# An RWKV-7 loop on TensorE: the source's order in turns, small tiles ahead of full ones, recurrence steps in two halves

## The chip, the cores and the metric

The kernel runs on one core of a Trainium2 chip. The metric is the device time of one execution in microseconds (us), as a median over runs. Two small networks are computed one after the other: a first block of two layers (an RWKV-7 mixer and a gated delta-rule mixer, each with a gated feed-forward part) and a second block of two layers. The change touches only the RWKV-7 mixer of the first layer, which takes about 280 us of the 2128 us span.

## The reference

For 256 tokens, a width of 1024 and 16 heads of 64, cut to what matters:

```python
r, k, v = lerp(0) @ w_rkv[0], lerp(1) @ w_rkv[1], lerp(2) @ w_rkv[2]
w_log = -softplus(-(w0 + tanh(lerp(3) @ w1) @ w2)) - 0.5
a = sigmoid(a0 + (lerp(4) @ a1) @ a2)
g = sigmoid(lerp(5) @ g1) @ g2
kk = l2norm(heads(k * k_k));  k = k * (1 + (a - 1) * k_a)
decay = exp(-exp(w_log))

def step(S, inp):                       # over the tokens, per head, S is 64x64
    sa = einsum('bhvk,bhk->bhv', S, a_t)            # a_t = -kk, b_t = kk * a
    S = S * w_t + sa * b_t + v_t * k_t
    return S, einsum('bhvk,bhk->bhv', S, r_t)

y = group_norm(y) * gn_g + gn_b;  y = (y + sum(r * k * r_k) * v) * g
return y @ w_out
```

The kernel does the recurrence in chunks of 64 tokens: within a chunk a triangular 64x64 matrix is inverted, and only the state S goes from chunk to chunk.

## The kernel before

The 16 heads are 8 pairs, p = 0 to 7. A pair fills 128 partitions, one head on rows 0 to 63 and one on rows 64 to 127, and its 256 tokens are 4 chunks. Each pair passes five stages, written as Python generators in `rwkv` (line numbers of before):

- `project(p)`: k, r and v of the pair, 24 matmuls of 128x128 by 256 each, all into the one PSUM bank `pj`; ScalarE copies a finished sum out (`ksb`, `rsb`, `vsb`, L1059) before the next may start. Each weight block arrives as f32, ScalarE casts its high half `wh` and VectorE subtracts for the low half `wl`.
- `stage_a(p)`: gates, norms and decays, mostly on VectorE and ScalarE, with single matmuls into the one bank `pt` (`lo0`, `kq`, `pr`), then four pairs of transposes into the same bank (`bh`, `kh`, `ah`, `vsb` against `ident`, L1136). After each pair four copies take the bank out (`bt`, `kt`, `at`, `vt`, L1143), in turn by VectorE, ScalarE, VectorE and ScalarE. Last come the products of 64x64 tiles into bank `G` (L1158).
- `stage_b(p)`: the inverse of the triangular matrices in 10 rounds, each 8 matmuls of 64x64 tiles into one of two banks `B` (L906) followed by one VectorE operation that the next round reads (`ivz` L921 or `ivx` L932), then three more products (`akv`, `WT`, `U`).
- `stage_c(p)`: the recurrence over 4 chunks. Per chunk `C<-st,WT` (L1201), VectorE's `sa` (L1203), products into `S` and `C` that read `sa`, and VectorE's new state `st` (L1217, L1221); then the group norm and the gate (`y`, `yq`, `lo1`).
- `early()`: the output projection over the pairs 0 to 5 (L1326), and `tail()`: vectors for later layers (`onecol`, `adacc`).

`run_spread` interleaves the generators: each has a number of steps and a start and end in units of one pair, and the generator whose next step is due first runs up to its next `yield`. A scheduler then takes these instructions in the program's order as priority and orders each engine's queue by its own estimate of durations, TensorE's too. Each engine runs its queue strictly in that order. A tile of a PSUM bank may be written again only when all reads of its last content are done.

TensorE works with two kinds of tile here: full ones (128 rows) and 64x64 ones, on which the two heads of a pair sit in two corners. The short products of `lo0` use 64 rows by 128 columns. Each f32 matmul stands in the trace as two records, so that a round of 8 matmuls is "x16" there.

Of the kernel before, what the change touches and what calls it, by code (L numbers as in the profile page):

```python
# [18 lines left out]
NCH = 8  # L19
# [732 lines left out]

def run_spread(*gens):

    live = [[g, n, a, b, 0] for g, n, a, b in gens]
    while live:
        e = min(live, key=lambda e: e[2] + (e[3] - e[2]) * (e[4] + 1) / e[1])
        try:
            next(e[0])
            e[4] += 1  # L760
        except StopIteration:
            live.remove(e)


class First:
# [174 lines left out]
    def rwkv(self):  # L940
        n, nc, P, T = self.n, self.n.nc, self.n.P, T1
        tc = n.tc
        with ExitStack() as es:
# [102 lines left out]
            def project(c, names="krv"):  # L1046
                for nm in names:
                    L = {"k": Lk, "r": Lr, "v": Lv}[nm]
                    ps = n.ps("pj", T)
                    w = n.wblock("r" + nm, c)  # L1050
                    for k in range(NCH):
                        wh, wl = w(k)
                        with tc.issue_after(self.anchor) if self.anchor is not None and k % 2 < 0 else nullcontext():
                            for i, (a, b) in enumerate(((wh, L[k][0]), (wh, L[k][1]), (wl, L[k][0]))):
                                nc.tensor.matmul(ps, a, b, start=(k == 0 and i == 0), stop=(k == 7 and i == 2))  # L1055
                        if k < 7 and nm not in "":
                            yield
                    o = st[c][nm] = t_(nm + "sb", 2)
                    nc.scalar.copy(o, ps)  # L1059
                    yield  # L1060

            def stage_a(c):
# [5 lines left out]
                for i, nm in enumerate(("SW", "AI")):  # L1068
                    w = slice(64 * i, 64 * i + 64)
                    ps = n.ps("pt", T)  # L1070
                    n.mm3([ps], [lambda k: tuple(q[w] for q in wa2)], [tuple(q[w] for q in lo[0])])
                    t = t_(nm)
                    sigmoid(t, ps, hc[:, i * 8 + c:i * 8 + c + 1])
                    SA.append(t)
                SW, A = SA
                yield
                q = t_("kq")
# [7 lines left out]
                nc.vector.scalar_tensor_tensor(kk, d["k"], P("k_k", c), rn, op0=MUL, op1=MUL)  # L1085
                yield
                cs = t_("cs")
# [16 lines left out]
                nc.scalar.activation(E0, dp, AF.Exp, scale=-KP)  # L1104
                yield
                kp_ = t_("kp")
# [13 lines left out]
                d["AR"] = AR4  # L1120
                yield
                r, v = d["r"], d["v"]
                nc.vector.tensor_tensor(AR4[:, :, 1], c4(r), c4(E1), op=MUL)
                pr = t_("pr")
                nc.vector.scalar_tensor_tensor(pr, r, P("r_k", c), kp_, op0=MUL, op1=MUL)
                yield
                ps = n.ps("pt", T)
                nc.tensor.matmul(ps, bo, pr, start=True, stop=True)
                bv = d["bv"] = r_(6, "bv")
                nc.vector.scalar_tensor_tensor(bv, ps, 64.0, v, op0=MUL, op1=MUL)  # L1130
                yield

# [13 lines left out]
                tok(lambda J: bh[:, ts(J, 128)], "bt", 2)  # L1146
                yield
                tok(lambda J: kh[:, ts(J, 128)], "kt", 2)
                yield
                tok(lambda J: ah[:, ts(J, 128)], "at", 2)  # L1150
                yield
                tok(lambda J: v[:, ts(J, 128)], "vt", 3)
# [16 lines left out]
            def stage_b(c):  # L1169
# [13 lines left out]

                akv = mm(d["Ak"], d["vt"], "akv")
                d["WT"] = mm(d["at"], XT, "WT")
                yield
# [3 lines left out]
            def stage_c(c):  # L1190
                d = st[c]
                yp = n.ps("S", T)
                S = None
                for j in range(4):
                    cj = ts(j, 64)
# [8 lines left out]
                    for r in H:  # L1204
                        nc.tensor.matmul(yp[r, cj], d["vt"][r, cj], d["Rk"][r, cj], start=True, stop=False)
                        if S is not None:
                            nc.tensor.matmul(yp[r, cj], S[r], d["AR"][r, j, 1], start=False, stop=False)
                        anchor = nc.tensor.matmul(yp[r, cj], sa[r], d["Rb"][r, cj], start=False, stop=True).ins
                    if j < 3:
                        ps = n.ps("C", 64)  # L1210
                        for r in H:
                            nc.tensor.matmul(ps[r], d["kt"][r, cj], d["vt"][r, cj], start=True, stop=False)
                            nc.tensor.matmul(ps[r], d["bt"][r, cj], sa[r], start=False, stop=True)
                        S2 = t_("st", 2, 64)
                        fj = d["f"][:, j:j + 1]
# [6 lines left out]
                        S = S2  # L1222
                    yield
                y = t_("y")
                nc.scalar.copy(y, yp)
                ps = n.ps("S", T)
                nc.tensor.matmul(ps, bo, y, start=True, stop=True)
                nc.vector.tensor_tensor(y, y, ps, op=SUB)
                q = t_("yq")
                nc.scalar.activation(q, y, AF.Square)  # L1230
                ps = n.ps("S", T)
                nc.tensor.matmul(ps, bo, q, start=True, stop=True)
                nc.scalar.activation(q, ps, AF.Ln, bias=n.consts[64e-5])
                nc.scalar.activation(q, q, AF.Exp, scale=-0.5)
                nc.vector.scalar_tensor_tensor(y, y, P("gn_g", c), q, op0=MUL, op1=MUL)
                yield
                nc.vector.scalar_tensor_tensor(y, y, P("gn_b", c), d["bv"], op0=ADD, op1=ADD)
# [5 lines left out]
                n.split_to(*yo[c], y)  # L1243
                yield

# [19 lines left out]
            def after(g, key, *needs):  # L1265
                for q in needs:
                    while q not in have:
                        yield
                yield from g()
                have.add(key)  # L1270


            def tail():
                for _ in more:
                    yield
                have.add("more")

            da, oa, la = 1, 0.0, 1.285
            ob, lb, oc, lc = 1.108, 1.0, 1.886, 0.963
            of, lf, oe, le = 0.1, 1.272, 7.918, 2.446  # L1280
            om, lm = 0.247, 8.0
            have.add(("f", 0))
            run_spread((tail(), 8 * len(self.PARTS[0]) + 1, om, om + lm),
                       *((after(lambda p=p: project(p), ("f", p), ("f", p - 1)), 24, p - 1 + of, p - 1 + of + lf) for p in range(1, NCH)),
                       *((after((lambda p=p: stage_a(p)) if p else (lambda: first), ("a", p), ("f", p)), 12, p + oa, p + oa + la) for p in range(NCH)),
                       *((after(lambda p=p: stage_b(p), ("b", p), ("a", p)), 12, p + ob, p + ob + lb) for p in range(NCH)),
                       *((after(lambda p=p: stage_c(p), ("c", p), ("b", p)), 6, p + oc, p + oc + lc) for p in range(NCH)),
                       (after(early, "e", "more", ("a", 7), ("c", 5)), 56, oe, oe + le))
            xs = new_x("s{}h")
# [617 lines left out]
```

## Time and profile before

| | |
|---|---|
| median of 3 runs (lowest, highest) | 2125.14 us (2124.67, 2127.45) |
| the profiled execution, its span | 2129.63 us, 2127.8 us |
| TensorE busy over the span | 2066.7 us, 97% |
| VectorE, ScalarE busy | 1449.8 us (68%), 1102.5 us (52%) |
| share of TensorE in the chain that ended last | 86% |
| DMA, mean | 159 GB/s |

A busy TensorE is not one at its peak: the ends of matmuls are modelled, and a short wait between two of them can vanish inside a busy stretch. So the starts of neighbouring matmuls are the better measure, and the text reads those.

### The profile page before, as it was taken

What the parts mean: (1) busy time and instruction counts of PE and PEld (TensorE: products, weight loads), DVE (VectorE), ACT (ScalarE), POOL (GpSimd) and SP (SyncE); (2) the same over time, 40 slices, a digit from 0 to 9 for tenths busy, and PEclk for the clock granted to TensorE, in tenths of its full rate; (3) what the DMA queues carried; (4) which work ended last, traced back from release to release, by engine and by line L of the source; (5) the groups of instructions that cost most, each with busy time, mean ns of one, the idle gap of its engine ahead of it and who ended that gap; (6) DMA issues with size and microseconds to landing.
All of it is one profiled execution on the core that took longest, in us unless ns stands there. A gap on an engine that the chain in (4) does not pass through costs nothing.

```text
span 2127.8 us, 43221 instructions
## 1 busy us (share of the span) xinstructions
PE 2066.7 (97%) x17602; PEld 1913.9 (90%) x17602; DVE 1449.8 (68%) x2959; ACT 1102.5 (52%) x2057; POOL 29.1 (1%) x68
## 2 busy tenths in 40 slices
PE   7999999999999999999999999999999999999998
PEld 6888888999888989999999876899999998779998
DVE  7878876887788867656555776755565457767555
ACT  4544445444745556545454744644454537456443
POOL 0000000000011100000000000000000000000000
PEclk9999999999999999999999999999999999999999
DMA  7524323896534337655554331455455443225553
GB/s 272 166 85 124 103 66 101 322 316 224 184 129 131 103 105 244 204 172 179 188 176 161 135 99 55 134 187 171 163 167 186 165 166 132 90 70 178 189 179 120
DMA packets 102087, 337.30 MB, mean 159 GB/s; under 512 B 11456, under 2 KB 19456, under 8 KB 101888
## 3 DMA queue, kind: packets, MB, share of 16 engines
q1 hardware_dynamic: 101888, 334.54, 47.2%
q8 instruction: 138, 2.26, 0.4%
q14 instruction: 61, 0.50, 0.1%
HBM read 333.45 MB, written 1.05 MB: 157 GB/s over the span
## 4 chain that ended last, share of the span: by engine, by line
PE 86%; DVE 6%; ACT 4%; DMA 2%; issue 1%; POOL 0%; SPq 0%; ACTq 0%; DVEq 0%; POOLq 0%
PE pj L157 17%; PE pj L158 17%; PE pj L160 17%; PE pj L128 9%; PE pj L1055 4%; PE B L906 2%; DVE wl L101 2%; PE yp L585 1%; PE B L1354 1%; PE pj L148 1%; DMA wr<-in_ffn_in_dram 1%; PE G L1158 1%; PE pj L149 1%; PE pj L152 1%; PE sy L638 1%
## 5 line engine op out<-in xcount | busy, mean ns | idle before, releaser
L101 DVE TENSOR_TENSOR wl<-wr,wh 128x1024 fp32r<-128x1024 f32 (+2 forms) x557 | 640.7, 1160 | 290.6 <-ACT wh L100 140.9
L100 ACT CAST wh<-wr 128x1024 fp32r<-128x1024 f32 (+2 forms) x557 | 555.0, 1002 | 495.6 <-PE pj L158 209.2
L266 DVE TENSOR_TENSOR hh<-sg,pj 128x256 f32<-128x256 f32 (+1 forms) x132 | 56.4, 428 | 147.4 <-PE pj L160 127.2
L817 DVE SCALAR_TENSOR_TENSOR adacc<-adar,cond,adacc 128x512 f32<-128x512 f32 x140 | 104.2, 744 | 11.3 <-DMA adar<-in_ada_dram 9.7
L177 ACT ACTIVATE q<-r 128x256 f32<-128x256 f32 (+1 forms) x80 | 33.1, 423 | 95.2 <-DVE r L198 71.1
L157 PE MATMUL pj<-s0h,wh 128*128 128x256 f32 (+1 forms) x240 | 68.4, 285 | 0.9 <-ACT wh L100 0.9
L160 PE MATMUL pj<-s6h,wl 128*128 128x256 f32 (+1 forms) x240 | 68.6, 286 | 0.0
L158 PE MATMUL pj<-s5l,wh 128*128 128x256 f32 (+1 forms) x240 | 68.4, 285 | 0.0
L157 PE MATMUL pj<-s6h,wh 128*128 128x256 f32 (+1 forms) x240 | 68.4, 285 | 0.0
L158 PE MATMUL pj<-s7l,wh 128*128 128x256 f32 (+1 forms) x240 | 68.3, 285 | 0.0
L160 PE MATMUL pj<-s1h,wl 128*128 128x256 f32 (+1 forms) x240 | 68.3, 284 | 0.0
L160 PE MATMUL pj<-s5h,wl 128*128 128x256 f32 (+1 forms) x240 | 68.2, 284 | 0.0
L160 PE MATMUL pj<-s7h,wl 128*128 128x256 f32 (+1 forms) x240 | 68.2, 284 | 0.0
L160 PE MATMUL pj<-s0h,wl 128*128 128x256 f32 (+1 forms) x240 | 68.2, 284 | 0.0
L160 PE MATMUL pj<-s4h,wl 128*128 128x256 f32 (+1 forms) x240 | 68.2, 284 | 0.0
L157 PE MATMUL pj<-s4h,wh 128*128 128x256 f32 (+1 forms) x240 | 68.2, 284 | 0.0
L158 PE MATMUL pj<-s1l,wh 128*128 128x256 f32 (+1 forms) x240 | 68.1, 284 | 0.0
L160 PE MATMUL pj<-s2h,wl 128*128 128x256 f32 (+1 forms) x240 | 68.1, 284 | 0.0
L158 PE MATMUL pj<-s3l,wh 128*128 128x256 f32 (+1 forms) x240 | 68.0, 284 | 0.0
L157 PE MATMUL pj<-s7h,wh 128*128 128x256 f32 (+1 forms) x240 | 68.0, 284 | 0.0
L157 PE MATMUL pj<-s1h,wh 128*128 128x256 f32 (+1 forms) x240 | 68.0, 283 | 0.0
L157 PE MATMUL pj<-s5h,wh 128*128 128x256 f32 (+1 forms) x240 | 68.0, 283 | 0.0
(1660 smaller groups left out, 7294.5 us busy)
## 6 DMA issues: line engine op xcount, KB each, us to landing
wr<-in_ffn_in_dram SPq DMA_DIRECT2D x264, 512.0 KB, 3.9
wr<-in_ffn_out_dram SPq DMA_DIRECT2D x96, 512.0 KB, 3.5
adar<-in_ada_dram SPq DMA_DIRECT2D x80, 512.0 KB, 4.6
wr<-in_w_in_dram SPq DMA_DIRECT2D x40, 512.0 KB, 3.4
wr<-in_ffn_out_dram SPq DMA_DIRECT2D x48, 384.0 KB, 3.6
wr<-in_gin_dram SPq DMA_DIRECT2D x32, 512.0 KB, 3.5
ada<-in_ada_dram SPq DMA_DIRECT2D x16, 512.0 KB, 7.4
wr<-in_w_out_dram SPq DMA_DIRECT2D x16, 512.0 KB, 3.5
```

The source lines that it names most:

```text
L100: nc.scalar.copy(h, r)
L101: nc.vector.tensor_tensor(l, r, h.bitcast(F32), op=SUB)
L128: mm(o, a, b[:, t0:], start=(c == 0), stop=(c == 23))
L148: mm(o, wh, xs[k][0], start=(i == 0), stop=False)
L157: mm(o, wh, xs[k][0], start=(i == 0), stop=False)
L158: mm(o, wh, xs[k][1], start=False, stop=False)
L160: mm(o, w(k)[1], xs[k][0], start=False, stop=(i == K - 1))
L177: nc.scalar.activation(q[k], d[k], AF.Square)
L266: nc.vector.tensor_tensor(hh, sg, up, op=MUL)
L817: nc.vector.scalar_tensor_tensor(acc, r[:, ts(k, 512)], c, acc, op0=MUL, op1=ADD)
L906: self.anchor = nc.tensor.matmul(out[r, c], lhsT[r, c], rhs[r, c], start=start, stop=start or b == nblk - 1).ins
L1055: nc.tensor.matmul(ps, a, b, start=(k == 0 and i == 0), stop=(k == 7 and i == 2))
```

## The change

Four things change. TensorE's queue in the loop is no longer ordered by the scheduler but stands as the source emits it (`manual_schedule`). `run_spread` gets `turns=12`: due times are rounded down to twelfths of a pair, and within one such turn the generators whose next step is marked as one of 64x64 tiles (a plain `yield` before it) run ahead of those marked `yield True` (full tiles). Steps are cut anew: a recurrence chunk becomes two steps, with `sa` between them, and the group norm and the first part of `stage_a` are cut into more steps. And the products with `kt` and `vt` use bank `dm` in place of `C` for the pairs 0 to 5. The number of matmuls stays the same.

```diff
-def run_spread(*gens):
-
-    live = [[g, n, a, b, 0] for g, n, a, b in gens]
+def run_spread(*gens, turns=None):
+    live = [[g, n, a, b, 0, None] for g, n, a, b in gens]
+    at = lambda e: e[2] + (e[3] - e[2]) * (e[4] + 1) / e[1]
     while live:
-        e = min(live, key=lambda e: e[2] + (e[3] - e[2]) * (e[4] + 1) / e[1])
+        e = min(live, key=at if turns is None else lambda e: (math.floor(at(e) * turns), e[5] is not None))
         try:
-            next(e[0])
+            e[5] = next(e[0])
             e[4] += 1
...
                         if k < 7 and nm not in "":
-                            yield
+                            yield True
...
+                    if i == 0:
+                        yield True
                 SW, A = SA
-                yield
+                yield True
...
                 akv = mm(d["Ak"], d["vt"], "akv")
+                yield
                 d["WT"] = mm(d["at"], XT, "WT")
...
+                other = "dm" if c < 6 else "C"
...
-                        anchor = nc.tensor.matmul(yp[r, cj], sa[r], d["Rb"][r, cj], start=False, stop=True).ins
                     if j < 3:
-                        ps = n.ps("C", 64)
+                        ps = n.ps(other, 64)
                         for r in H:
                             nc.tensor.matmul(ps[r], d["kt"][r, cj], d["vt"][r, cj], start=True, stop=False)
+                    if S is not None:
+                        yield
+                    for r in H:
+                        if j < 3:
                             nc.tensor.matmul(ps[r], d["bt"][r, cj], sa[r], start=False, stop=True)
+                    for r in H:
+                        nc.tensor.matmul(yp[r, cj], sa[r], d["Rb"][r, cj], start=False, stop=True)
...
-                    yield
+                    yield True if j == 3 else None
                 y = t_("y")
                 nc.scalar.copy(y, yp)
+                yield True
...
-            ob, lb, oc, lc = 1.108, 1.0, 1.886, 0.963
+            ob, lb, oc, lc = 1.108, 13 / 12, 1.886, 1.0
...
+            with tc.manual_schedule(engines={mybir.EngineType.PE}):
+                run_spread(*((after(lambda p=p: stage_c(p), ("c", p), ("b", p)), 12, p + oc, p + oc + lc) for p in range(NCH)),
+                           *((after(lambda p=p: stage_b(p), ("b", p), ("a", p)), 13, p + ob, p + ob + lb) for p in range(NCH)),
+                           *((after((lambda p=p: stage_a(p)) if p else (lambda: first), ("a", p), ("f", p)), 13, p + oa, p + oa + la) for p in range(NCH)),
+                           *((after(lambda p=p: project(p), ("f", p), ("f", p - 1)), 24, p - 1 + of, p - 1 + of + lf) for p in range(1, NCH)),
+                           (tail(), 8 * len(self.PARTS[0]) + 1, om, om + lm),
+                           (after(early, "e", "more", ("a", 7), ("c", 5)), 56, oe, oe + le), turns=12)
```

Three places of TensorE's queue show the order. A row is a line of the kernel, the operation, out<-in by the names above, and the size of the result; line numbers of the changed kernel are 3 to 17 higher. The first place is the middle of the loop, around pair 3, where the recurrence and the inverse of neighbouring pairs run beside `project`. Before:

```order
L1080 MATMUL pt<-kq,bo 128x256
L906 MATMUL B<-ivz,ivt 64x64 x8
L1055 MATMUL pj<-s4l,wh 128x256
L1055 MATMUL pj<-s4h,wl 128x256
L1205 MATMUL S<-Rk,vt 64x64
L1055 MATMUL pj<-s5h,wh 128x256
L1201 MATMUL C<-st,WT 64x64 x2
L1207 MATMUL S<-AR,st 64x64
L1055 MATMUL pj<-s5l,wh 128x256
L906 MATMUL B<-ivx,MT 64x64 x8
L1055 MATMUL pj<-s5h,wl 128x256
```

The same stage with the change:

```order
L1208 MATMUL C<-st,WT 64x64 x2
L1212 MATMUL S<-Rk,vt 64x64
L1214 MATMUL S<-AR,st 64x64
L1212 MATMUL S<-Rk,vt 64x64
L1214 MATMUL S<-AR,st 64x64
L909 MATMUL B<-ivx,MT 64x64 x8
L1058 MATMUL pj<-s6h,wh 128x256
L1058 MATMUL pj<-s6l,wh 128x256
L1058 MATMUL pj<-s6h,wl 128x256
L1225 MATMUL S<-Rb,sa 64x64 x2
L909 MATMUL B<-ivz,ivt 64x64 x8
L1058 MATMUL pj<-s7h,wh 128x256
```

Before, the kind of tile changes 8 times in 11 rows, now 3 times in 12: the 64x64 rows of a turn stand together. The second place is the pair of transposes of `kh` and the next, of `ah`, into the same bank `pt`, for pair 3. Before:

```order
L1136 MATMUL pt<-ident,kh 128x128 x2
L1055 MATMUL pj<-Mset,wh 128x256
L906 MATMUL B<-ivt,ivz 64x64 x8
L1179 MATMUL B<-vt,Ak 64x64 x8
L1055 MATMUL pj<-Mset,wl 128x256
L1179 MATMUL B<-ivt,at 64x64 x7
L1136 MATMUL pt<-ident,ah 128x128 x2
```

And now, with the rows that follow:

```order
L1141 MATMUL pt<-ident,kh 128x128 x2
L1058 MATMUL pj<-L6h,wh 128x256
L1058 MATMUL pj<-L6l,wh 128x256
L1058 MATMUL pj<-L6h,wl 128x256
L909 MATMUL B<-ivx,MT 64x64 x8
L1141 MATMUL pt<-ident,ah 128x128 x2
L1058 MATMUL pj<-L7h,wh 128x256
L1058 MATMUL pj<-L7l,wh 128x256
L1058 MATMUL pj<-L7h,wl 128x256
L1058 MATMUL pj<-Mset,wh 128x256 x2
```

Between the two pairs of transposes 25 rows' worth of matmuls stood (23 small, 2 full), and 11 stand there now (8 small, 3 full). The last two rows are the third place: the sum of r ends with `L7h,wl` and that of v begins with `Mset,wh`, into the one bank `pj`, with nothing between. Before, the same border of pair 3 was:

```order
L906 MATMUL B<-ivx,MT 64x64 x8
L1055 MATMUL pj<-L7h,wl 128x256
L1158 MATMUL G<-AR,bh 64x128 x3
L1055 MATMUL pj<-Mset,wh 128x256 x2
L1158 MATMUL G<-AR,bh 64x128 x2
```

Three products into `G` stood between the two sums there. Over the whole loop, from the first `lo0` row to the last `lo1` row, the kind of tile on TensorE changes 344 times before and 263 times with the change.

## Rows read from the trace of the kernel before

**Rows 1.** Windows, the loop: length, busy us (instructions) of each engine, granted clock, DMA share.
```profile
51.70:334.30 282.60, 277.54 (x3524) 230.49 (x3523) 221.05 (x585) 133.39 (x342) 0.00 (x0) 0.99 0.35 111
```

**Rows 2.** Timeline of TensorE: start, length, line, out<-in, tile, count; two rounds.
```profile
316.21 0.28 PE L1326 MATMUL pt<-yo0l,wh 128*128 128x256 f32 x1
316.42 0.68 PE L906 MATMUL B<-ivt,ivz 64*64 64x64 f32 x16
316.93 0.63 PE L1179 MATMUL B<-vt,Ak 64*64 64x64 f32 x16
317.49 0.39 PE L1326 MATMUL pt<-yo0h,wl 128*128 128x256 f32 x1
317.71 0.28 PE L1326 MATMUL pt<-yo1h,wh 128*128 128x256 f32 x1
317.83 0.28 PE L1326 MATMUL pt<-yo1l,wh 128*128 128x256 f32 x1
```

**Rows 3.** Timeline of TensorE, a recurrence chunk between full tiles.
```profile
321.33 0.28 PE L1326 MATMUL pt<-yo4h,wl 128*128 128x256 f32 x1
321.54 0.33 PE L1201 MATMUL C<-st,WT 64*64 64x64 f32 x4
321.70 0.28 PE L1205 MATMUL S<-Rk,vt 64*64 64x64 f32 x2
321.82 0.28 PE L1207 MATMUL S<-AR,st 64*64 64x64 f32 x2
322.02 0.38 PE L1326 MATMUL pt<-yo5h,wh 128*128 128x256 f32 x1
322.25 0.28 PE L1326 MATMUL pt<-yo5l,wh 128*128 128x256 f32 x1
```

**Rows 4.** Timeline of all engines, one round of the inverse; brackets: idle before, releaser.
```profile
161.09 0.68 PE L906 MATMUL B<-ivx,MT 64*64 64x64 f32 x16
...
161.82 0.42 DVE L921 TENSOR_TENSOR ivz<-B,rc 128x256 f32<-128x256 f32 x1 [0.23 <-PE B L906]
...
163.98 0.42 DVE L932 TENSOR_TENSOR ivx<-B,ivx 128x256 f32<-128x256 f32 x1
...
164.46 0.54 PEld L906 LDWEIGHTS B<-ivx,MT 64*64 64x64 f32 x14 [0.34 <-DVE ivx L932]
```

**Rows 5.** Groups of VectorE, 75 to 330 us: count, busy us, mean ns, idle before.
```profile
L921 DVE TENSOR_TENSOR ivz<-B,rc 128x256 f32<-128x256 f32 x40 | 16.8, 421 | 7.0 <-PE B L906 6.8
...
L1203 DVE TENSOR_TENSOR sa<-C,U 128x64 f32<-128x64 f32 x24 | 5.2, 218 | 5.8 <-PE C L1201 5.5
...
L1221 DVE SCALAR_TENSOR_TENSOR st<-C,f,sf 128x64 f32<-128x64 f32 x16 | 4.5, 282 | 7.4 <-PE C L1213 7.2
```

**Rows 6.** Timeline, bank pt between the transposes of kh and ah.
```profile
166.69 0.38 PE L1136 MATMUL pt<-ident,kh 128*128 128x128 f32 x2
...
167.45 0.28 DVE L1143 COPY kt<-pt 64x128 f32<-64x128 f32 x1
167.76 0.26 ACT L1143 COPY kt<-pt 64x128 f32<-64x128 f32 x1 [2.71 <-DVE kt L1143]
168.30 0.29 DVE L1143 COPY kt<-pt 64x128 f32<-64x128 f32 x1
168.71 0.26 ACT L1143 COPY kt<-pt 64x128 f32<-64x128 f32 x1
...
169.11 0.44 PE L1136 MATMUL pt<-ident,ah 128*128 128x128 f32 x2
```

**Rows 7.** Timeline, bank pj between the sums of r and v.
```profile
161.70 0.39 PE L1055 MATMUL pj<-L7h,wl 128*128 128x256 f32 x1
...
162.12 0.37 ACT L1059 COPY rsb<-pj 128x256 f32<-128x256 f32 x1 [2.78 <-PE pj L1055]
...
162.59 0.19 PEld L1055 LDWEIGHTS pj<-Mset,wh 128*128 128x128 f32 x1 [0.17 <-ACT rsb L1059]
```

**Rows 8.** Windows, a stretch at a lower granted clock.
```profile
132.00:140.00 8.00, 8.00 (x75) 6.40 (x76) 3.99 (x9) 1.60 (x5) 0.00 (x0) 0.57 0.24 76
```

More of the change, by code (lines that the diff above doesn't have):

```diff
@@ L1085, in stage_a @@
                 nc.vector.scalar_tensor_tensor(kk, d["k"], P("k_k", c), rn, op0=MUL, op1=MUL)
-                yield
+                yield True
                 cs = t_("cs")
@@ L1104, in stage_a @@
                 nc.scalar.activation(E0, dp, AF.Exp, scale=-KP)
-                yield
+                yield True
                 kp_ = t_("kp")
@@ L1120, in stage_a @@
                 d["AR"] = AR4
-                yield
+                yield True
                 r, v = d["r"], d["v"]
@@ L1125, in stage_a @@
                 nc.vector.scalar_tensor_tensor(pr, r, P("r_k", c), kp_, op0=MUL, op1=MUL)
-                yield
+                yield True
                 ps = n.ps("pt", T)
@@ L1130, in stage_a @@
                 nc.vector.scalar_tensor_tensor(bv, ps, 64.0, v, op0=MUL, op1=MUL)
-                yield
+                yield True
                 def tok(src, name, bufs):
@@ L1146, in stage_a @@
                 tok(lambda J: bh[:, ts(J, 128)], "bt", 2)
-                yield
+                yield True
                 tok(lambda J: kh[:, ts(J, 128)], "kt", 2)
-                yield
+                yield True
                 tok(lambda J: ah[:, ts(J, 128)], "at", 2)
-                yield
+                yield True
                 tok(lambda J: v[:, ts(J, 128)], "vt", 3)
@@ L1207, in stage_c @@
                             nc.tensor.matmul(yp[r, cj], S[r], d["AR"][r, j, 1], start=False, stop=False)
[L1208 removed]
                     if j < 3:
[L1210 removed]
+                        ps = n.ps(other, 64)
                         for r in H:
                             nc.tensor.matmul(ps[r], d["kt"][r, cj], d["vt"][r, cj], start=True, stop=False)
+                    if S is not None:
+                        yield
+                    for r in H:
+                        if j < 3:
                             nc.tensor.matmul(ps[r], d["bt"][r, cj], sa[r], start=False, stop=True)
+                    for r in H:
+                        nc.tensor.matmul(yp[r, cj], sa[r], d["Rb"][r, cj], start=False, stop=True)
+                    if j < 3:
                         S2 = t_("st", 2, 64)
@@ L1222, in stage_c @@
                         S = S2
-                    yield
+                    yield True if j == 3 else None
                 y = t_("y")
                 nc.scalar.copy(y, yp)
+                yield True
                 ps = n.ps("S", T)
@@ L1230, in stage_c @@
                 nc.scalar.activation(q, y, AF.Square)
+                yield True
                 ps = n.ps("S", T)
@@ L1235, in stage_c @@
                 nc.vector.scalar_tensor_tensor(y, y, P("gn_g", c), q, op0=MUL, op1=MUL)
-                yield
+                yield True
                 nc.vector.scalar_tensor_tensor(y, y, P("gn_b", c), d["bv"], op0=ADD, op1=ADD)
@@ L1243, in stage_c @@
                 n.split_to(*yo[c], y)
-                yield
+                yield True
             gk, gr, gv = lerps(1, "s", Lk), lerps(0, "L", Lr), lerps(2, "M", Lv)
@@ L1282, in rwkv @@
             have.add(("f", 0))
[L1283 to L1288, printed above, removed]
+            with tc.manual_schedule(engines={mybir.EngineType.PE}):
[5 more added lines that the diff above has]
+                           (after(early, "e", "more", ("a", 7), ("c", 5)), 56, oe, oe + le), turns=12)
             xs = new_x("s{}h")
```

## The prediction

> **What bounds the kernel now.** The change stays inside the RWKV loop, so I read the windows first: from the first `lo0` row to the last `lo1` row is 51.8 to 334.2 us, 282.4 us in which TensorE is busy 277.5 us, VectorE 221 and ScalarE 133 [rows 1]. TensorE sets this stretch; VectorE, at 78%, is not far behind. But a busy TensorE is not one at its peak, so I then read the timeline by starts. In a stream, full rows of 256 columns start 0.12 us apart (317.71, 317.83), and a round of sixteen 64x64 records takes 0.51 us, 0.03 each [rows 2]. What does not stream is the border between the kinds of tile. From the full row at 316.21 to the full one at 317.71 are 1.50 us; one full row (0.12), 32 small records (0.96) and another full row (0.12) make 1.20, so going into the small tiles and back costs 0.30 [rows 2]. From 321.33 to 322.25 are 0.92 us with two full rows and 8 small records, 0.48 in all: 0.44 for both borders [rows 3]. So a border costs 0.15 to 0.22 us, and I take 0.19. With 344 borders in the loop that is 65 us of its 282.
>
> Priced like this, row by row along the queue of before (other shapes by their own starts), the loop holds 206.6 us of matmuls and 65.4 us of borders, 272.0 in all. The stretch took 282.4, so 10.4 us are left for waits. A third of these have one place: from 132 to 140 us the granted clock is 0.57, that is, much of it at 1.2 instead of 2.4 GHz, and 8 us at 0.57 lose 3.4 us [rows 8].
>
> **The change, part by part.** *Borders.* The same matmuls now have 263 borders, 81 fewer: 81 x 0.19 = 15.4 us gained (12.2 to 17.8 by the two bounds). This lies on TensorE itself, so nothing hides it.
>
> The Trainium skill ("TensorEngine Tiling (Array Packing)", Key Properties) says that a change of tiling mode drains TensorE, and its page "TensorE: Matmul & The Clock Gate" (Single matmul latency) gives an isolated matmul a constant of 398 cycles at 2.4 GHz, 166 ns. An estimate from that page makes the gain 81 x 0.166 = 13.4 us; the rows say 0.19, and the sum goes by the rows.
>
> *Gaps.* The other side is the fixed order. Before, the queue was laid out so that the next reader of a bank or of a VectorE result came about when it was ready; now it comes when its turn comes, and all behind it on TensorE waits too. So I count, for each pair of rows of which the second must wait for VectorE or ScalarE to work on the first's result, the priced matmuls that stand between (the cover), and compare it with what the trip needs. The needs, from the nominal end of the first row to the start of the second:
> - A round of the inverse: sixteen records from 161.09 end nominally at 161.57; `ivz` starts at 161.82, takes 0.42, and `ivx` reaches TensorE 0.06 us after its end (164.40 to 164.46): 0.25 + 0.42 + 0.06 = 0.73 us [rows 4, 5]. `sa` and `st` by the same hops, with 0.22 and 0.28 us of VectorE: 0.53 and 0.59 [rows 5].
> - The bank `pj`: `L7h,wl` starts at 161.70, ScalarE copies 0.37 us, the next sum starts at 162.59. That is 0.77 us after a nominal end at 161.82; the row is 0.11 longer than one in a stream, and from that end it is 0.66. I take 0.70 [rows 2, 7].
> - The bank `pt` after transposes: four copies in turn on two engines, 1.09 us of work; the next pair starts 2.42 us after the first, 2.24 after its nominal end (0.18 for two) [rows 6]. Half of that is queueing; matmuls 0.38, copies 1.09 and five hops of about 0.04 leave 1.5 without any. I take the middle, 1.86, since VectorE's queue is as full as before.
> - The other trips (`G`, `y`, `yq`, `pr`, `onecol`, `lo0`, `kq`) in the same way, 0.45 to 1.17 us.
>
> To all of these but the transposes I add 0.1 us for a queue at VectorE or ScalarE (0 and 0.2 are the bounds). Where a shortfall lies within the gap of another, it is counted once. Counted so, the queue of before falls short by 5.1 us in 19 places; with the 3.4 us of clock that is 8.5 of the 10.4 us left above, so the count is a fair measure.
>
> The queue of the changed kernel falls short in 53 places, by 25.9 us:
> - Transposes, 17 places, 11.2 us. From `kh` to `ah` the eight covers are 0.36, 0.36, 2.06, 1.22, 1.22, 1.70, 1.70 and 0.86 us against 1.86 (before none was under 2.0), from `ah` to `vsb` 0.72 to 1.58 but for one. The new steps put one pair of transposes into each turn, and a turn is too short for four copies.
> - The inverse, 9 places, 3.6 us: for the first and the last pair two or three rounds stand in one turn, with a cover of nothing; elsewhere only three full rows stand between two rounds, a cover of 0.74 to 0.81 us against 0.83.
> - The bank `pj`, 4 places, 3.2 us: where a turn runs two steps of `project`, one sum follows the last with a cover of nothing. ScalarE's copy is then exposed whole.
> - The recurrence, 8 places, 3.5 us: mostly at the ends of the loop. In its middle the half steps do what they are for: `sa` and `st` mostly get covers of 1.0 to 2.2 us.
> - The rest, 15 places, 4.4 us: `G` from `bh` to `kh` 1.35, `y` to `yq` 1.1, `onecol` to `pr` 1.1 (cover nothing, twice), others 0.85.
>
> What is queued behind such a wait is everything on TensorE; in the queue of before a `project` row could have stood there.
>
> *No cost.* The bank `dm`, idle until `early` needs it, only frees `C`. The added Python steps issue nothing. The weights' loads stand in almost the same order on SP's queue, with DMA at 35% in the loop [rows 1]; if one came late, a turn would wait some 1 us for the cast, and I put it into the range.
>
> *Sum.* -15.4 for the borders, +25.9 - 5.1 = +20.8 for the waits: **+5.4 us**. The clock's 3.4 us I leave as they are. All durations are of the profiled execution, 2129.63 us with a span of 2127.8, which becomes 2135.0; the median of the runs shown is 2125.14, 4.5 below, and I carry the difference over: 2130.5, **2131 us**.
>
> Bounds: with no queueing and 1.5 for the transposes the shortfalls are 17.3 against 3.6, and the sum is -1.7 us; with 0.2 of queueing and 2.24 they are 36.9 against 8.0, and it is +13.5. The border's bounds move it by +3.2 or -2.4. So the forecast itself spans 2123 to 2140. A change under 0.2%, 4.3 us, can't be told from none.
>
> **The rivals.**
> *Faster: the copies keep pace.* VectorE and ScalarE are ordered by program order too, and the steps of a turn now stand near the front of it; a copy or a round's operation may find its engine free each time, and a wait in one gap gives time to all others. For it: VectorE stood idle for TensorE 6.8 us before its 40 `ivz` [rows 5]. Against it: the four copies are a chain over two queues, and in the shown trip ScalarE waits for VectorE [rows 6]. Without the transposes' share the sum is 5.4 - 11.2 = -5.8, without that of the inverse and the recurrence too -12.9: 2112 to 2119 us. It decides when less than 16.2 of the 25.9 us arises (15.4 + 5.1 - 4.3).
> *Even.* The low bounds hold: trips at their bare length, 17 to 19 us of shortfall, 2123 to 2129 us.
> *Slower by more: the clock.* The one stretch at 0.57 lies where the trace's waits bunch; more waits could bring more such stretches, each worth 3.4 us [rows 8]. Three of them on top of the forecast give 2130.5 + 10.2, 2141 us. By the Trainium skill ("TensorE: Matmul & The Clock Gate", Part 1) the clock follows how busy TensorE has lately been. The stretch of rows 8 does not speak against it.
>
> **How the numbers follow.** The forecast, waits beyond the saved borders, gets 0.45; the clock on top of it 0.10; even 0.18; faster 0.27. Slower by over 0.2% is then 0.55, the same 0.18, faster 0.27. The range, 2113 to 2143, leaves out the far end of the faster case (the borders alone, 2110) and of the clock's.
>
> **What would show it.** In the changed profile the loop should take 287.8 us in place of 282.4. Borders: 263, at 0.3 to 0.44 us for two; if two cost half of that, the gain was mis-sized. Gaps: TensorE waits for ScalarE's `kt` and `at` before `ident,ah` and `ident,vsb`, about 0.6 us each, for `ksb` or `rsb` four times at the border of two sums, and for `ivz` or `ivx` nine times. If these rows show no such waits and the loop is shorter than 275 us, my needs were too long and the faster rival is right. If the waits are there but the loop holds further ones for weights or `bh`, I missed chains of several operations. A granted clock of 0.5 in more places than one would be the third rival.

## The result, and the profile after

The changed kernel takes 2152.57 us as a median of 4 runs (2150.35 to 2153.01), against 2126.3 us (2124.67 to 2130.62, 4 runs) before: a ratio of 1.0109, 95% interval 1.0093 to 1.0126. It is slower by 1.1%, some 23 us; the forecast had the sign and a fifth of the size, and the time lies 9.6 us above the range. The profiled execution has a span of 2151.1 us, 23.3 more than before, and 23.0 of them arise inside the loop, from the first `lo0` row (52.62 us) to the last `lo1` row (357.97 us): 305.4 us where it took 282.4.

The windows view of that stretch, in the columns of [rows 1]:

```profile
52.50:358.10 305.60, 269.43 (x3531) 228.61 (x3531) 227.18 (x586) 133.84 (x343) 0.00 (x0) 0.96 0.33 104
```

VectorE and ScalarE work hardly longer than before (227 us against 221, and 134 against 133). TensorE is busy for 8 us less, and the stretch is 23 us longer: it stands still, openly now. Its mean granted clock fell from 0.99 to 0.96. What it waits for shows the view of waits, TensorE alone, in the loop (who waits <- for whom: us in total, times, longest; waits of over 0.15 us are named):

```profile
PE pt L1141 <- ACT kt L1148: 8.6, 6, 1.9
PE pt L1141 <- ACT bt L1148: 4.5, 5, 1.6
PE pj L1058 <- ACT rsb L1062: 3.8, 3, 1.7
PE B L909 <- DVE ivz L924: 3.5, 7, 1.0
PE B L909 <- DVE ivx L935: 3.2, 5, 1.3
PE S L1247 <- ACT yq L1244: 2.4, 3, 1.3
PE pt L1141 <- ACT at L1148: 2.4, 3, 1.0
PE pt L1133 <- DVE pr L1130: 2.0, 1, 2.0
```

Summed over all rows this named idle time is 35.5 us; before it was 3.9. The transposes lead with 15.5. One of their trips, in the timeline of all engines:

```profile
213.64 0.44 PE L1141 MATMUL pt<-ident,kh 128*128 128x128 f32 x2 [1.55 <-ACT bt L1148]
...
213.87 1.21 DVE L101 TENSOR_TENSOR wl<-wr,wh 128x1024 fp32r<-128x1024 f32 x1
...
214.36 0.68 PE L1184 MATMUL B<-ivt,at 64*64 64x64 f32 x16
...
215.12 0.28 DVE L1148 COPY kt<-pt 64x128 f32<-64x128 f32 x1
...
215.32 0.73 DVE L820 SCALAR_TENSOR_TENSOR adacc<-adar,cond,adacc 128x512 f32<-128x512 f32 x1
215.49 0.26 ACT L1148 COPY kt<-pt 64x128 f32<-64x128 f32 x1
...
216.09 0.29 DVE L1148 COPY kt<-pt 64x128 f32<-64x128 f32 x1
...
216.42 0.26 ACT L1148 COPY kt<-pt 64x128 f32<-64x128 f32 x1 [0.67 <-DVE kt L1148]
216.73 0.29 PEld L1141 LDWEIGHTS pt<-ident,ah 128*128 128x128 f32 x2 [1.83 <-ACT kt L1148]
```

The reader is to see what stands between: the bank is full at 213.8 us, but VectorE has a weight split, `wl`, of 1.21 us in front of the first copy, and an `adacc` of 0.73 between the first and the third. The trip took 2.91 us where the prediction allowed 1.86. In [rows 6] it took 2.24, with 25 rows of work laid into it where 11 stand here, so that TensorE did not wait. Trips as such are not longer now: from the start of a pair of transposes to the end of its last copy the 32 trips of before take 2.75 us in the mean (1.9 to 4.4), those of the changed kernel 2.46 (1.7 to 3.8). What is gone is the work laid into them.

The bank `pj` in the same way, with ScalarE's weight cast in front of the copy:

```profile
178.72 0.28 PE L1058 MATMUL pj<-L7h,wl 128*128 128x256 f32 x1
...
178.92 1.05 ACT L100 CAST wh<-wr 128x1024 fp32r<-128x1024 f32 x1 [0.76 <-PE pj L1058]
...
179.99 0.26 ACT L1148 COPY at<-pt 64x128 f32<-64x128 f32 x1
...
180.27 0.37 ACT L1062 COPY rsb<-pj 128x256 f32<-128x256 f32 x1
...
180.70 0.50 PE L1058 MATMUL pj<-Mset,wh 128*128 128x256 f32 x2 [1.70 <-ACT rsb L1062]
```

From 178.72 to 180.70 are 1.98 us, where the same border took 0.89 in [rows 7]: the cast of 1.05, and behind it a copy `at` of 0.26, stand in front of `rsb` and make the difference. And the clock, in windows (columns as in [rows 8]); these are four of the seven places where it fell:

```profile
114.00:118.00 4.00, 4.00 (x43) 3.54 (x43) 2.38 (x8) 0.78 (x3) 0.00 (x0) 0.57 0.58 185
182.00:186.00 4.00, 4.00 (x41) 3.48 (x37) 1.87 (x5) 1.03 (x4) 0.00 (x0) 0.57 0.51 175
216.00:220.00 4.00, 3.27 (x27) 2.93 (x27) 2.25 (x6) 0.99 (x4) 0.00 (x0) 0.57 0.50 149
312.00:316.00 4.00, 3.76 (x50) 3.36 (x50) 1.59 (x7) 0.89 (x3) 0.00 (x0) 0.57 0.36 102
```

Each stands right behind waits of TensorE or begins within one: 1.8 us at 112.9, 1.7 at 180.7, 1.7 at 216.7, and 0.8 and 0.95 at 309.7 and 311.7. The loop in windows of 4 us, each counted with 4 x (1 - granted clock), lost 11.9 us to the lower of the two levels; before, 3.4.

### The profile page after: what moved, and what is told of

Its sections match the earlier page's. It is cut to its first block, busy times and chain, and to the rows that moved or that the text cites. A ratio compares the mean times of both kernels' runs of the same rounds, so it can differ in the third digit from the quotient of the medians.

```text
span 2151.1 us, 43248 instructions
## 1 busy us (share of the span) xinstructions
PE 2058.2 (96%) x17602; PEld 1911.2 (89%) x17602; DVE 1454.6 (68%) x2959; ACT 1101.9 (51%) x2057; POOL 29.0 (1%) x68
## 3 DMA queue, kind: packets, MB, share of 16 engines
HBM read 333.45 MB, written 1.05 MB: 156 GB/s over the span
## 4 chain that ended last, share of the span: by engine, by line
PE 66%; DVE 5%; ACT 3%; DMA 1%; issue 1%; POOL 0%; ACTq 0%; DVEq 0%; SPq 0%; POOLq 0%
PE pj L157 15%; PE pj L158 15%; PE pj L160 15%; PE pj L128 8%; DVE wl L101 2%; PE yp L585 1%; PE B L1369 1%; PE pj L148 1%; PE pj L149 1%; PE pj L152 1%; PE sy L638 1%; PE S L546 1%; DMA wr<-in_ffn_in_dram 1%; ACT wh L100 1%; DVE r L214 1%
## 5 line engine op out<-in xcount | busy, mean ns | idle before, releaser
L820 DVE SCALAR_TENSOR_TENSOR adacc<-adar,cond,adacc 128x512 f32<-128x512 f32 x140 | 104.3, 745 | 13.2 <-DMA adar<-in_ada_dram 11.7
```

What stands on the lines that cost most here:

```text
L820: nc.vector.scalar_tensor_tensor(acc, r[:, ts(k, 512)], c, acc, op0=MUL, op1=ADD)
```

## Experiments

For every run the table gives the ratio to the kernel before, measured beside it (its own median was 2126 to 2131 us in these groups of runs, so times are compared by ratios), and from its profile: the loop (`lo0` to `lo1`) in us, the borders along its queue, the named idle time of TensorE in it, the us lost at half clock, and the rest, that is, what the loop changed against before (282.4; 344 borders; 3.9; 3.4) beyond idle time and clock.

| kernel | ratio (95%) | loop | borders | idle | clock | rest |
|---|---|---|---|---|---|---|
| changed | 1.0109 (1.0093 to 1.0126) | 305.4 | 263 | 35.5 | 11.9 | -17.1 |
| e1 scheduler | 1.0001 (0.9988 to 1.0015) | 285.2 | 315 | 10.4 | 6.8 | -7.1 |
| e2 due order | 1.0122 (1.0094 to 1.0150) | 305.9 | 292 | 31.3 | 13.7 | -14.2 |
| e3 three engines in order | 1.0874 (1.0851 to 1.0898) | 467.8 | 263 | 125.5 | 107.6 | |
| e4 two banks | 1.0035 (1.0020 to 1.0050) | 287.4 | 263 | 21.2 | 5.1 | -14.0 |
| e5 no adacc | 1.0094 (1.0060 to 1.0127) | 298.4 | 263 | 30.7 | 8.6 | -16.0 |
| e6 before, two banks | 0.9972 (0.9959 to 0.9985) | 275.7 | 322 | 3.7 | 1.7 | -4.8 |
| e7 fixed middle, two banks | 0.9984 (0.9971 to 0.9998) | 280.3 | 290 | 13.2 | 1.7 | -9.7 |
| e8 steps alone | 0.9994 (0.9980 to 1.0007) | 280.5 | 336 | 8.2 | 1.7 | -4.5 |
| e9 small splits | 1.0099 (1.0079 to 1.0120) | 301.3 | 263 | 28.3 | 15.4 | -17.5 |
| e10 small splits, no adacc | 1.0033 (1.0017 to 1.0048) | 286.8 | 263 | 24.4 | 1.7 | -14.4 |
| e11 as e7, empty step | 0.9990 (0.9975 to 1.0005) | 278.0 | 284 | 13.0 | 1.7 | -11.8 |
| e12 fixed order alone | 1.0248 (1.0223 to 1.0273) | 326.5 | 256 | 43.1 | 15.4 | -7.1 |
| e13 two banks, no filler | 0.9988 (0.9972 to 1.0005) | 283.5 | 263 | 14.6 | 8.6 | -14.8 |
| e14 copies on one engine | 1.0068 (1.0046 to 1.0090) | 289.7 | 263 | 26.0 | 3.4 | -14.8 |
| e15 before, two banks, one engine | 0.9966 (0.9952 to 0.9980) | 271.3 | 311 | 2.8 | 0.0 | -6.6 |

The theory, formed from the profile after: the fixed order exposes trips, and filler work in VectorE's and ScalarE's queues (`wl`, `wh`, `adacc`) makes them longer than allowed. Its rivals were that the steps and turns are at fault, or the bare chain of copies.

**e1: the scheduler orders TensorE again.**

```diff
-            with tc.manual_schedule(engines={mybir.EngineType.PE}):
+            with nullcontext():
```

> The changed kernel, but the scheduler orders TensorE again (turns, new steps, banks and constants stay). The queue has 315 borders in the loop, against 263 with the fixed order and 344 before. Theory 'fixed order': the waits (35.5 us of named idle time on TensorE in the changed kernel, 3.9 before) come from TensorE's order being fixed; they fall to about 4 us, the half-clock stretches to one, and the 29 borders fewer than before give 29 x 0.19 = 5.5 us: about 2121 us. Rival 'steps': the new steps and turns also give VectorE and ScalarE a worse order, and waits of over 10 us stay: 2135 us or more.

The whole loss is gone: the same as before. So it is the fixed order. The 2121 us did not come, and the rival's waits of over 10 us did (10.4, of which 3.5 for weight splits), though not its 2135 us. That it is not 5 us faster lies not in the borders (rest -7.1 for 29 fewer) but in 6.5 us of new idle time and 3.4 of clock in the profiled execution, the slowest of ten.

**e2: no turns; e12: only the fixed order, on the kernel before.**

```diff
-                           (after(early, "e", "more", ("a", 7), ("c", 5)), 56, oe, oe + le), turns=12)
+                           (after(early, "e", "more", ("a", 7), ("c", 5)), 56, oe, oe + le), turns=None)
```

> The changed kernel without turns: TensorE in the source's order, generators by due time alone. 292 borders in the loop in place of 263 (+29, +5.5 us). If the sorting within turns makes the waits (rounds and transposes once a turn), they fall from 35 to under 15 us and the time to 2135 us or less. If the fixed order as such makes them, they stay at 30 us or more: 2150 to 2160 us. A count of the covers along the two queues gives 22.7 against 27.6 us of shortfall, that is, 2153 us.

> The kernel before with TensorE in the source's order and nothing else: old steps, no turns, no bank dm. 256 borders (88 fewer, -17 us). Along its queue the count of covers gives 47.9 us of shortfall, against 27.6 in the changed kernel and 5.1 before. Theory: the fixed order is what costs, and the turns and half steps win part of it back, so this one is slower than the changed kernel, 2165 us or more. Rival: turns and half steps do not help, and this one is at 2150 or less.

Without turns nothing is better: 1.0122 and 1.0109 can't be told apart, so that the turns by themselves win nothing that the runs show. The fixed order alone is the worst of the three, 2.5% over before: the new steps, with the bank and the order of the generators that come with them, win back about half of what it costs. In e12 `yq` waits at every pair (7.8 us in 8 places); the changed kernel, with `y` and `yq` in steps of their own, has 2.4 there.

**e8: the steps alone.** Neither fixed order nor turns.

> The kernel before with the new steps, the half steps of the recurrence, bank dm and the new constants, but neither turns nor a fixed order (336 borders). Prediction's view: it costs nothing and brings nothing, 2124 to 2133 us. If the emission order that feeds VectorE's and ScalarE's queues is worse by itself, it is slower by 5 us or more.

The same as before: the steps, bank `dm` and the constants cost nothing.

**e3: VectorE and ScalarE in the source's order too.**

```diff
-            with tc.manual_schedule(engines={mybir.EngineType.PE}):
+            with tc.manual_schedule(engines={mybir.EngineType.PE, mybir.EngineType.DVE, mybir.EngineType.Activation}):
```

> The changed kernel with VectorE and ScalarE in the source's order too, so that no weight split (wl 1.2 us, wh 1.05 us) or adacc (0.74 us) that the source has elsewhere stands between two copies of one bank. Theory 'filler': such work, put there by the scheduler, is what makes the trip over the bank of the transposes 2.4 to 3.6 us; in source order it is 1.6 to 1.9 us, the transposes' waits halve and the whole is 2135 to 2142 us. Rival 'order of TensorE': the trips stay over 2.2 us, since the source has as much work between; 2150 us. Rival 'heads of queues': the engines now stand at the source's next operation whether it is ready or not, and waits grow: 2160 us or more.

A miss for the theory; the last of the three cases came, far beyond its 2160 us: 187 us slower. In the view of waits of its loop, TensorE alone:

```profile
PE pj L1058 <- ACT wh L100: 69.0, 20, 6.4
PE pj L1058 <- DVE wl L101: 12.3, 21, 1.7
```

In the timeline ScalarE stands 4.16 us before its copy `vsb` (99.66 us), waiting for TensorE, and the cast of the next weights comes behind it, at 99.93: in source order a cast stands behind operations that wait themselves. By this place and the 69.0 us above, the filler has to come early, and where the scheduler puts it early it stands in front of copies.

**e4: two banks for the transposes.**

```diff
-                other = "dm" if c < 6 else "C"
+                other = "C"
...
-                    ps = n.ps("pt", T)
+                    ps = n.ps({"bt": "pt", "kt": "dm", "at": "pt", "vt": "dm"}[name], T)
```

> The changed kernel with the transposes in turn in banks pt and dm, and the products with kt and vt in C as before. A pair of transposes then waits for the copies of the pair two turns earlier. Theory 'bank': the 16.6 us of waits at the transposes fall under 3 us, and of the 11.9 us lost at half clock the stretches that follow such waits (at 73, 113, 216 and 280 us) go, 5 to 7 us; the recurrence pays up to 4 us for C: 2133 to 2140 us. Rival 'copies': what waits now for the bank then waits for the copies' results or for work behind them on VectorE (G, ivz, rsb), and the gain is under 5 us: 2148 us or more.

Groups of TensorE's instructions in its loop; idle time stands behind the bar:

```profile
L1141 PE MATMUL pt<-ident,ah 128*128 128x128 f32 x16 | 3.7, 316 | 0.5 <-ACT bt L1148 0.4
L1141 PE MATMUL dm<-ident,kh 128*128 128x128 f32 x16 | 3.6, 308 | 0.0
```

The transposes' 15.5 us (the expectation's 16.6) are 0.4, and the loop is 18.0 us shorter: 14.3 by idle time, 6.8 by the clock, while other terms take 3 back. By the starts 1.7 of these 3 are a price that the recurrence pays for `C`: a step of 0.26 to 0.35 us from one 64x64 row to the next that writes `C`, where 0.05 is usual, stands in 12 places where 4 were, too short to be named. The named waits hardly moved on: those of the recurrence rose from 1.1 us to 2.8. By the ratios two thirds of the whole loss (0.74 of 1.09%) hang on this one bank. What is left of the clock's loss lies in the first pair, before 88 us.

**e5, e9, e10: the filler taken away.** e5 leaves out most of `adacc`, e9 makes the weight splits small, e10 does both; TensorE's order is that of the changed kernel in all three.

```diff
+                        if l == 0 and part in (2, 3, 4) and q + k > 0:
+                            pass
```

```diff
-        nc.scalar.copy(h, r)
-        nc.vector.tensor_tensor(l, r, h.bitcast(F32), op=SUB)
+        s = slice(0, 128 if name in ("rk", "rr", "rv") else n)
+        nc.scalar.copy(h[:, s], r[:, s])
+        nc.vector.tensor_tensor(l[:, s], r[:, s], h[:, s].bitcast(F32), op=SUB)
```

> The changed kernel, with 42 of the 48 multiply-adds into adacc (0.74 us each on VectorE, 31 us) left out of the loop, so that the vectors that they make for later layers are not computed; TensorE's order is unchanged. Theory 'filler': these operations stand between the four copies of a bank and ahead of ivz and ivx; the trips over the transposes' bank fall from 2.7 us in the mean to 1.7 to 2.0, the named waits from 35.5 us to under 25, and the loop from 305 us to 290 or less. Rival 'chain': the trip is long from its own four copies and hops, the weight splits take the place of adacc in front of them, and the loop stays over 300 us.

> The changed kernel, in which the weight splits of the loop treat only the first 128 of a block's 1024 columns (wh about 0.3 us in place of 1.05 on ScalarE, wl 0.28 in place of 1.22 on VectorE) and all eight column blocks use them, so that the projections are computed with one eighth of their weights; TensorE's order and all loads are unchanged. Theory 'splits': a whole split stands in front of a copy or of ivz and is the larger part of the waits; the named idle time falls from 35.5 us to under 20, the sums' bank from 4.9 to under 2, and the loop from 305 to 285 us or less. Rival 'chain': the trips are long from their own four copies; idle time stays over 28 us and the loop over 297.

> Both left out, seven eighths of the weight splits in the loop and 42 of 48 multiply-adds into adacc, so that neither the projections nor the later layers' vectors are those of the reference. What waits are left belong to the order of TensorE and to the chains themselves. The prediction's count without any queueing, 17 us (transposes at 1.5 us), should then come out: named idle time of 12 to 18 us, loop of 275 to 283 us. If filler was not the cause of the mis-sized waits it stays over 25 us.

Each one alone gives 5 to 7 us of idle time, less than its theory wanted, and by its ratio can't be told from the changed kernel; both together give 11.1, and the loop 18.6, of which 10.2 are the clock's. (From the nominal end of a pair of transposes to the start of the next, the mean trip of the changed kernel is 2.44 us over the 23 under 4 us, not 2.7; it falls to 2.33, 2.19 and 1.97.) In e10 the waits for the transposes are still the largest:

```profile
PE pt L1146 <- ACT kt L1153: 6.9, 6, 2.0
PE B L914 <- DVE ivz L929: 2.8, 5, 1.0
PE S L1252 <- ACT yq L1249: 2.1, 2, 1.3
PE pt L1146 <- ACT at L1153: 2.1, 3, 0.8
```

24.4 us is more than the 12 to 18 expected, and just under the 25 at which the theory would have failed. But not all filler is gone in e10: the eight splits of the output projection (`wh` 0.83 us, `wl` about 0.95) stay whole. From the first of them on (277.1 us in the changed kernel, 260.7 in e10) the idle time is 9.8 us in both kernels; ahead of it, it falls from 25.7 us to 14.6. So filler is at least a third of the idle time, 14.6 us are there without it, and what the last 9.8 us owe to it was not tested.

**e14: all four copies on ScalarE.**

```diff
-                            cp = nc.scalar.copy if h else nc.vector.tensor_copy
+                            cp = nc.scalar.copy
```

> The changed kernel with all four copies after a pair of transposes on ScalarE (same bank, same order of TensorE). Theory 'alternation': each of three changes of engine in a chain waits for the other engine's queue, 1.2 us wl or 0.74 us adacc on VectorE; on one engine a trip is 1.4 us plus at most one cast of 1.05, mean trip from 2.7 to under 2, transposes' idle time from 15.5 to under 8 us, loop 290 to 297 us. Rival: ScalarE, with the casts in front, is as late, and idle time stays over 13.

Nearly as the theory said: the transposes' idle time is 6.1 us, the mean trip 2.01, the loop 289.7. By the ratios only 0.4 of 1.09% come back, since the profiled execution was the fastest of three, by 6.5 us and at the highest clock. The largest group is halved:

```profile
L1141 PE MATMUL pt<-ident,ah 128*128 128x128 f32 x16 | 3.5, 300 | 4.0 <-ACT kt L1148 4.0
```

**e13: two banks and no filler.** The edits of e4 and e10 together.

> Two banks for the transposes, and seven eighths of the loop's weight splits and 42 of 48 multiply-adds into adacc left out (neither the projections nor the later layers' vectors are those of the reference), TensorE in the changed kernel's fixed order. If bank trip and filler are the two causes, the transposes' idle time (10.3 us in the run without filler) goes and 12 to 15 us of named idle time stay, mostly inverse and first pair; the loop is 273 to 278 us. If the waits only move on, it stays over 284.

The idle time came as expected, 14.6 us, with none at the transposes; the loop did not (283.5), as 8.6 us went to the clock in this execution (its eight spread from 2121 to 2134 us, at granted clocks of 0.992 to 0.986). The two causes account for 21 of the 35.5 us; what is left is inverse (3.6), the bank `pj` (3.3), recurrence (2.5), and single waits of the first and last pair.

**e7, e11: the fixed order in the middle only, two banks.** `run_spread` is cut at due times 1.4 and 7.5, and only what lies between is emitted inside `manual_schedule`; e11 adds an empty step:

```diff
                     nc.scalar.copy(o, ps)
                     yield True
+                    yield True
```

> The changed kernel with two banks for the transposes, and TensorE's order fixed only in the middle (due times 1.4 to 7.5 pairs); the scheduler orders the first pair and the last ones, where there is little other work to put into a gap. 290 borders. In the fixed run with two banks the waits over 0.25 us before 91 us and after 278 us add up to 8 and 7 us, and its 5 us at half clock lie all before 88 us. Theory 'cover': those 15 us and the clock's 5 go, 27 borders come back (+5 us): 2137 - 20 + 5 = 2122 us, under both kernels. Rival: the stretch's ends are bound by chains, whoever orders them; then 2132 to 2137 us.

> Fixed order in the middle and two banks, as in the run before of that kind, and an empty step of project after each sum, so that the next sum begins more often in a later turn. Its pj waits were 5.7 us in 7 places; they should fall to about 2 us, 284 borders in place of 290 give 1 us more: about 2121 to 2123 us, 0.3% under before. If ScalarE's copy is late by a weight cast whatever stands between, the waits stay and it is 2126 us again.

e7 is 0.16% under before, less than hoped: its ends got better (idle 21.2 to 13.2 us), but the gap to before is small. e11 is not the 0.3% under before that was expected, and can't be told from e7: the waits at `pj` fell from 4.3 us of idle time to 1.9, yet those of the inverse rose from 4.1 to 6.5.

**e6, e15: two banks on the kernel before**, the scheduler ordering; e15 also with the edit of e14.

> The kernel before, with the transposes in turn in banks pt and dm and nothing else changed (322 borders). The scheduler's order had only 1.0 us of named waits at the transposes, so the bank itself is worth at most that, and 22 borders fewer give 22 x 0.19 = 4.2 us if borders are what counts: 2121 to 2126 us, just under before. If borders in the scheduler's queue are hidden by waits that come instead (as the 29 fewer of the first run brought nothing), it is the same as before within 0.2%.

> The kernel before with two banks for the transposes and all their copies on ScalarE: 32 copies less on VectorE per quarter of the loop, 18 us of its 221 in all, 311 borders against 322. The scheduler's order hides the trips already, so only the borders (11 x 0.16 = 1.8 us) and the emptier VectorE count: 2118 to 2123 us, 0.3 to 0.5% under before. If ScalarE's copies come late behind casts, it is 2126 or more.

(There are 64 such copies on VectorE in the whole loop; "per quarter" was a slip.) Both beat both kernels: 0.9972 and 0.9966, 6 to 7 us; between the two the runs do not tell. The windows of their loops:

```profile
52.40:328.30 275.90, 271.65 (x3524) 228.19 (x3524) 220.65 (x584) 133.45 (x343) 0.00 (x0) 0.99 0.35 114
```

```profile
53.70:325.20 271.50, 268.24 (x3523) 225.77 (x3523) 205.97 (x520) 148.08 (x407) 0.00 (x0) 1.00 0.35 116
```

Idle time could not fall much (3.9 us before, 3.7 and 2.8 now). With a second bank the scheduler has more freedom and leaves 22 and 33 borders fewer; the rest of -4.8 and -6.6 us is their price.

## Why the prediction was wrong

**Borders: right.** 15.4 us were forecast (12.2 to 17.8), and the rest is -17.1. That is a remainder, but the starts give the same: without named waits and half clock, the steps from one row to the next across a border add up to 70.2 us before (344) and to 50.8 now (263), 19.4 less, and the steps within one kind of tile to 2.2 us more. The last column repeats it: divided by the borders saved it is 0.17 to 0.27 us in thirteen of the fifteen kernels whose rest is given, seven of them with the same 263 borders; only e8 (8 borders) and e12 (0.08) stand apart. In e12 the steps across borders save as much (49.0 us are left of 70.2), but the uncut chunks of the recurrence take back about 5 of the 11 us that are missing: in 24 of them TensorE waits for `sa`, in 6 long enough to be named; in 18 the second row here starts 0.32 us after the first, where it is 0.06 at most before.

```profile
152.64 0.28 PE L1207 MATMUL S<-AR,st 64*64 64x64 f32 x2
153.02 0.27 PE L1208 MATMUL S<-Rb,sa 64*64 64x64 f32 x1
```

A pair of borders by itself costs less. In the timeline of the changed kernel, TensorE:

```profile
267.54 0.28 PE L1058 MATMUL pj<-s7h,wl 128*128 128x256 f32 x1
267.75 0.33 PE L1225 MATMUL S<-Rb,sa 64*64 64x64 f32 x4
267.91 0.63 PE L909 MATMUL B<-ivx,MT 64*64 64x64 f32 x16
268.48 0.39 PE L1058 MATMUL pj<-L0h,wh 128*128 128x256 f32 x1
```

0.94 us, less 0.12 and 20 x 0.03, are 0.22 for two. Rows of before gave 0.30 and 0.44 [rows 2, 3], and a border saved was worth 0.21 in the sum (17.1 by 81). That small delays beside a border went with it is my reading; of what they consist the runs don't show. The estimate from the Trainium skill ("TensorE: Matmul & The Clock Gate", Single matmul latency), 0.166 us each, lies between the bare price and that.

**Waits: the right stages, too small.** The step that failed is the allowance for the queues: "To all of these but the transposes I add 0.1 us for a queue at VectorE or ScalarE", and 1.86 us for the transposes "since VectorE's queue is as full as before". The forecast was 25.9 us; measured are 35.5: transposes 15.5 (forecast 11.2), inverse 6.7 (3.6), `pj` 4.9 (3.2), recurrence 1.1 (3.5, too much), all else 7.3 (4.4). Within the transposes the places differ: `ah` waits for `kt` 8.6 us, where seven covers fell short by 5.6; `vsb` waits in 3 places, where covers fell short in 7.

The 1.86 us were read from one trip and taken half way down to a bare 1.5 (the 0.74 us between are a third of its 2.24, not the half that the text calls queueing), though a queue as full as before would keep the whole. From the start of the pair to the end of the last copy, the 1.86 us are 1.99 (with 0.18 for the pair, less 0.05 to TensorE); the means of this are 2.75 before, 2.46 with the change and 1.94 in e10. There, with trips about as long as allowed, the transposes wait 10.3 us, about the forecast 11.2: so the count of covers held for them, and the trip's length was wrong. What is missing are operations of 0.74 to 1.23 us in front: taking most of them away gives 11.1 us, and 24.4 are left (10.3, inverse 4.7, `pj` 3.3, recurrence 1.2, all else 4.9). That this lies near the 25.9 is luck in part: the recurrence was forecast 2.3 us too high, the inverse 1.1 too low. Before, the same operations stood there; there the covers were long enough. The forecast's own upper bound (0.2 us and 2.24) gives 36.9 us, close to the 35.5.

**Clock: the step "The clock's 3.4 us I leave as they are".** It took 11.9 us, 8.5 more. This was the third rival, as a mechanism: given 0.10 and 10.2 us, where it belonged to the forecast itself, since the forecast multiplied the waits. Each of the seven stretches of the changed kernel follows waits of 0.8 to 2.0 us or begins within one. The Trainium skill's rule that the clock follows how busy TensorE has been ("TensorE: Matmul & The Clock Gate", Part 1) fits these seven. It is not shown by the stretch of before: that one does not lie "where the trace's waits bunch". It began at 132.6 us, and from 88.4 to 164 us no wait of TensorE is named. Shortly ahead of it, in the trace of before, TensorE is busy throughout at the full clock:

```profile
126.00:130.00 4.00, 4.00 (x59) 3.35 (x57) 3.36 (x10) 0.52 (x2) 0.00 (x0) 1.00 0.42 135
```

How much waiting brings a fall about, or what else does, no run here measured. Idle time and loss do not go in step either (e10: 24.4 and 1.7; e9: 28.3 and 15.4; e13: 14.6 and 8.6), and each of these losses is that of one execution.

With -17.1, +31.6 and +8.5 the loop's +23.0 is accounted for; against the forecast, waits and clock added 10.8 and 8.5 us, and borders took 1.7. The faster rival fails by its own test: not less than 16.2 us of shortfall arose but 35.5. **The parts called free were free**: e8 for the steps and `dm`; `early`, the weights' loads and DMA name no wait in the changed loop.

Open stays what of the 24.4 us in e10 is TensorE's order, what the splits left there, and what operations of the stages themselves in the queues (before the first `pr` of the changed kernel VectorE runs seven others of its stage in a row, `kk` to `ah`). Whether copies that two engines make independently would shorten the trip further was not tried.

## What to carry to other kernels

A fixed order is paid where a chain's trip is longer than the work laid into it: count the covers, and for the trip take not one that you happen to look at but all of its kind in the trace of before, with their spread (here 1.9 to 4.4 us), since one operation in front costs its whole length. Before ordering by hand, ask which resource makes the trip matter; here a second bank for the transposes was worth 16 us to the fixed order by the ratios (18 in the profiled loop), and with the scheduler's order it gave 0.3% under the kernel before. Order of TensorE and order of the engines that feed it belong together: fixing TensorE's alone with one bank for the transposes, or all three by the source, both lost.

## What was unexpected of the hardware

- The lower clock cost nothing in e15, 3.4 us before, 11.9 us in the changed kernel (seven stretches of 1.7 us of loss each) and 15.4 us in e9 and in e12. In the changed kernel it followed waits of no more than 2 us: after the wait of 1.8 us at 112.9 the granted clock is 0.57 over the 4 us from 114. In the kernel before it fell with no named wait in the 44 us ahead of it.
- Two borders of kinds of tile cost 0.22 us in a clean place, and about 0.2 each in the sum. In every kernel traced here the median start of a 64x64 row is 0.21 us after that of a full one, and of a full one 0.15 us after that of a 64x64 one; less 0.12 and 0.03, that is 0.21 for two.
